# Split-float projections of a transformer block on one core: low part of the moving side by adding DMA, sums on VectorE, reversed values on ScalarE's queue

## The chip, the cores and the metric

The kernel runs on one NeuronCore of a Trainium2 chip. It computes one layer of a hybrid block for 1024 tokens of width 1024 in float32. The metric is device time in microseconds, from the first to the last instruction of one launch, with the little that lies around them. The kernel before takes 2165.42 us, the median of three runs (2165.0 to 2167.76).

## The reference

All is float32. `SEQ` and `D_MODEL` are 1024, `FF_HIDDEN` is 2816; there are 8 heads in the gated recurrence (`hgrn2_mixer`) and 16 in the stick-breaking attention.

```python
h = rms_norm(x, norm1_gain[layer])
proj = h @ w_in[layer]
hq, hf, hi, hg, sq, sk, sv, ga, gb = split_cols(proj, IN_SPLITS)
o_hg = hgrn2_mixer(hq, hf, hi, lower_bounds[layer])
o_hg = rms_norm(o_hg, hg_out_norm[layer]).reshape(b, s, HG_WIDTH)
o_hg = o_hg * jax.nn.sigmoid(hg.astype(jnp.float32))
y_hg = o_hg.astype(x.dtype) @ w_hg_out[layer]
...
o_sb = stick_breaking(q, k, v).transpose(0, 2, 1, 3).reshape(b, s, SB_WIDTH)
y_sb = o_sb.astype(x.dtype) @ w_sb_out[layer]
mixed = jax.nn.sigmoid(ga) * y_hg + jax.nn.sigmoid(gb) * y_sb
x = x + mixed @ w_o[layer]
h2 = rms_norm(x, norm2_gain[layer])
gate, up = split_cols(h2 @ w_ffn_in[layer], (FF_HIDDEN, FF_HIDDEN))
x = x + (jax.nn.silu(gate) * up) @ w_ffn_out[layer]
```

## The kernel before

**Numbers in two parts.** Every large product splits its operands into a high part (a cast to float32r) and a low part (the value less its high part) and makes three matmuls: high by high, high by low, low by high (`mm3`). For each operand somebody must make the two parts. There are two ways in the kernel. `split` casts on ScalarE and subtracts on an engine that is named (VectorE or GpSimd). `load_w` casts on ScalarE, writes the negated high part of the value with a second ScalarE pass (L118, `wl`), and lets a DMA on GpSimd's queue add the raw value to it in SBUF (L119).

**Stages, in the order of the program.** (1) The input is normalized and turned (`norm_x`, `turn_x`), while the first head's weights arrive. (2) The recurrence: for each of 8 heads `hg_head` makes the head's own small matmuls, woven between the projections of the next head. Values (`v`) are needed with every second token tile reversed: `hg_v` stores the raw rows to `d_v`, `turn_v` copies them reversed inside DRAM to `d_vr`, `load_v` reads them back into the odd tiles of `v`; the matmuls of `state` (L464) read them. (3) The stick-breaking attention, woven with its projections and with the gates' projections. (4) Three products (`w_hg_out`, `w_sb_out`, `w_o`), in the class `Product`. (5) The feed-forward input (`ffn_in`), (6) its output (`ffn_out`).

**The three products.** Each is cut into quarters and made with seven block products in place of eight (`SEQ43`, `SEQ34`), with sums and differences of quarters on either side (`A_STEPS` and `B_STEPS`, made in place by `sum_step`). One block product is a *job*: four tiles of 12 matmuls each, in four PSUM banks. While job n runs, job n+1 is prepared, by four steps that stand behind the tiles of job n: `stationary(0)`, `moving(0)`, `moving(1)`, `stationary(1)`. A stationary half is 128 x 1024 values for two tiles, in buffers `wh` and `wl`; a moving half is 128 x 1024 values for half of the inner dimension, in two buffers `u` that hold the halves of one job together. The job's first tile reads both moving halves, the second half from its seventh matmul on. Sums for the stationary side run on GpSimd (`a_sum`), the others on VectorE. When a tile is done it is added up on VectorE (L941) or copied by ScalarE; finished quarters are multiplied by a gate (L969) that is loaded just before. The third product adds to the input (`add_x1`, L981).

**Into the feed-forward.** The second norm's rows are turned (`turn_h2`) in 16 turns, eight woven into the last job, eight behind the first four of `ffn_in`'s block products. A turn scales a row tile on VectorE (`hn`, L1058), transposes it on TensorE (L1062), copies it out, and makes its part of the moving operands at once (`b_op`): number 1 or 2 for the first four tiles, 5 or 6 for the last four. Numbers 7, 3 and 4 are made later in one go (`b_rest`). `a_prep` makes the weights' operands six block products ahead, with sums and half of the subtractions on GpSimd. `(f, m)` below is block product m of column block f; the order starts (0,1), (0,2), (1,1), (1,2), (2,1), (2,2), (0,5), (0,6), (1,5), (0,7), (0,3), (0,4).

**What sets the order.** TensorE's order is written out by hand (`weave`, `run`). The other engines' orders come from the framework's scheduler, and every engine and every DMA queue works strictly in its order: an instruction that waits holds all behind it. Loads go through SyncE's queue, the two `wr` buffers of the weights among them.

Of the kernel before, what the change touches and what calls it, by code (L numbers as in the profile page):

```python
# [7 lines left out]
F32 = mybir.dt.float32  # L8
# [3 lines left out]
AF = mybir.ActivationFunctionType  # L12
ALU = mybir.AluOpType
# [3 lines left out]
P = 128  # L17
# [17 lines left out]
def hybrid_block(ctx, tc, x, norm1_gain, w_in, lb_logits, hg_out_norm, sb_q_norm, sb_k_norm,  # L35
                 w_hg_out, w_sb_out, w_o, norm2_gain, w_ffn_in, w_ffn_out,
                 c_ident, c_blk, c_lvl, c_base, out):
    nc = tc.nc
# [64 lines left out]
    d_x1 = dp.tile([NT, P, D], F32, name="d_x1")  # L103
    d_act = dp.tile([3, NF // 2, P, HS], F32, name="d_act")

    def load_w(src, k0, nk, c0, ncol, pool=None):
        raw = wp.tile([P, nk, ncol], F32, tag="wr", bufs=2, name="wr")
        if pool:
            both = pool(F32R, (P, 2, nk, ncol))
            hi, lo = both[:, 0], both[:, 1]  # L110
        else:
            hi = wp.tile([P, nk, ncol], F32R, tag="wh", name="wh")
            lo = wp.tile([P, nk, ncol], F32R, tag="wl", name="wl")
        dma = nc.sync.dma_start(raw, src[k0 * P:(k0 + nk) * P, c0:c0 + ncol].rearrange("(k p) n -> p k n", p=P))
        if src is w_hg_out and c0:
            order(dma, last["oh"][7 if c0 == P else -1])
        nc.scalar.copy(hi, raw)
        nc.scalar.activation(lo, raw, AF.Copy, scale=-1.0)  # L118
        nc.gpsimd.dma_start(lo.bitcast(F32).rearrange("p k n -> p (k n)"), raw.rearrange("p k n -> p (k n)"),  # L119
                            accum_op=ALU.add)  # L120
        return hi, lo

    blocks, loaded = [], []
# [240 lines left out]
        return proj_v(get, evac)  # L364

    def turn_v(h):
        nc.sync.dma_start(d_vr[h // 2], d_v[h // 2, :, ::-1, :])

    def load_v(h):
        for j in range(2):  # L370
            nc.sync.dma_start(hd[h + j]["v"][:, 1::2, :], d_vr[h // 2, :, :, j * P:(j + 1) * P].rearrange("a p c -> p a c"))

    def hg_gates(h):
        d = hd[h]
# [14 lines left out]
    def hg_head(h):  # L389
# [3 lines left out]
        e = {}  # L393

        def prep():
            sc = e["sc"] = hg.tile([P, S], F32, tag="sc", bufs=1, name="sc")
            nc.gpsimd.memset(sc, 0.0)
            kb = e["kb"] = hg.tile([P, S], F32, tag="kl", name="kb")
            qb = e["qb"] = hg.tile([P, S], F32, tag="kl", name="qb")
            c4 = c.rearrange("p (b l) -> p b l", l=4)  # L400
            nc.gpsimd.tensor_sub(qb.rearrange("p (b l) -> p b l", l=4), c4,
                                 c4[:, :, 1:2].broadcast_to([P, S // 4, 4]))
# [114 lines left out]
        def norm(half):  # L517
# [7 lines left out]
            nc.sync.dma_start(d_ohg[h][:, sl], r)  # L525

        return prep, [
            (0.86, lambda: (base(0), turn_v(h) if h % 2 == 0 else None)),
            (2.463, lambda: (base(1), level_prep(0))),
            (2.075, lambda: (across(), level_prep(1), load_v(h) if h % 2 == 0 else None)),  # L530
            (2.243, lambda: (level(0), level_prep(2))),
            (0.5, lambda: turn(0)),
            (1.257, lambda: turn(1)),
# [333 lines left out]
    def split(e, src, hi, lo):  # L867
        nc.scalar.copy(hi, src)  # L868
        e.tensor_sub(lo, src, hi.bitcast(F32))  # L869
# [9 lines left out]
    class Product:  # L879
# [17 lines left out]
        def prep(self, i):  # L897
            m = self.seq[i]
            sides = self.ops[i] = [], []

            def stationary(c):
                cols = slice(c * 256, (c + 1) * 256)
                raw = lambda q: self.raw("a", q)[:, :, cols]
                hi = wp.tile([P, 4, 256], F32R, tag="wh", name="wh")
                lo = wp.tile([P, 4, 256], F32R, tag="wl", name="wl")
                sides[0].append((hi, lo))
                sum_step(self.a_sum, A_STEPS, m, raw)
                split(nc.vector, raw(A_SRC[m]), hi, lo)

            def moving(c):  # L910
                if c == 0:
                    sides[1].extend((unit1(), unit1()))
                ks = slice(2 * c, 2 * c + 2)
                raw = lambda q: self.raw("b", q)[:, ks, :]
                sum_step(nc.vector, B_STEPS, m, raw)
                split(nc.vector, raw(B_SRC[m]), *(u[:, ks, :] for u in sides[1]))
            return [lambda: stationary(0), lambda: moving(0), lambda: moving(1), lambda: stationary(1)]

        def tile(self, i, j):
            m = self.seq[i]  # L920
# [79 lines left out]
    def load_x1(t):  # L1000
        if t % 2 == 0:
# [5 lines left out]
    SEQ43, SEQ34 = (1, 2, 5, 6, 7, 4, 3), (1, 2, 5, 6, 7, 3, 4)  # L1007
    phases = [
        Product(SEQ43, w_quarter(w_hg_out, lambda: unit1, False), o_quarter(d_ohg, lambda: unit1),
                accumulate(m1, lambda: unit2, finish_hg), nc.gpsimd),  # L1010
        Product(SEQ43, w_quarter(w_sb_out, lambda: unit2, False), o_quarter(d_osb, lambda: unit1),
                accumulate(mixed, lambda: unit1, finish_sb), nc.gpsimd),
        Product(SEQ34, lambda q: mixed[q // 10 + q % 10 * 10], w_quarter(w_o, lambda: unit2, True), add_x1,
                nc.gpsimd)]
    jobs = [(ph, i) for ph in phases for i in range(7)]

    def job_steps(n):
        ph, i = jobs[n]
        box = []

        def start():
            for ph2, i2 in jobs[n + 2:n + 3]:
                ph2.load(i2)
            box.extend(jobs[n + 1][0].prep(jobs[n + 1][1]) if n + 1 < len(jobs) else [lambda: None] * 4)
        steps = [(0.0, start)]
        for j in range(4):
            steps += ph.tile(i, j) + [(0.0, lambda j=j: box[j]())]
        return steps

    phases[0].load(0)  # L1030
# [21 lines left out]
    def turn_h2(t, g):  # L1052
        half, j = t // 4, t % 4
        q = 11 + 10 * g + half
        if j == 0:
            h2f[q] = unit1(F32)
        hn = mp.tile([P, HS], F32, tag="m2", name="hn")
        nc.vector.scalar_tensor_tensor(hn, x1s(t, g * HS, HS), rss[t], g2[:, 0, g * HS:(g + 1) * HS],  # L1058
                                       op0=ALU.mult, op1=ALU.mult)
        tp = pbank("pt")  # L1060
        for i in range(4):
            nc.tensor.transpose(tp[:, i * P:(i + 1) * P], hn[:, i * P:(i + 1) * P], ident)  # L1062
# [55 lines left out]
    a_done = []  # L1118
# [206 lines left out]
```

## Time and profile before

The profiled execution took 2166.08 us, of which its span is 2164.3 us.

| what | value |
|---|---|
| median of three runs | 2165.42 us |
| profiled execution's own time | 2166.08 us |
| its span | 2164.3 us |
| mean granted TensorE clock | 0.986 |
| VectorE busy | 1430.1 us (66%) |
| ScalarE busy | 1107.9 us (51%) |
| GpSimd busy | 627.6 us (29%) |
| moved by DMA | 228.96 MB |

How to read it: PE is TensorE's matmuls, PEld its weight loads, DVE is VectorE, ACT is ScalarE, POOL is GpSimd, SP is SyncE; a name with q behind it is the engine's queue. "pd L138 <- DVE u L869" is a matmul into tile pd, line 138, that waited until the VectorE instruction of line 869 into tile u was done; then come the total in us, how often, and the longest. In a timeline a row has the start and the length in us, engine, line, operation, tile written <- tiles read, sizes, and in brackets the engine's idle time before it and what ended that. In a table by windows a row has the stretch, its length, each engine's busy time with its instructions, the granted clock of TensorE (1.00 is full) and the busy share of the 16 DMA engines.

### The profile page before, as it was taken

The numbers are of one execution on the slowest core, as the hardware profiler recorded it, in microseconds if no ns is written. First come the engines' busy times: TensorE is split into PE (matmuls) and PEld (weight loads), VectorE is DVE, ScalarE is ACT, GpSimd is POOL, SyncE is SP. The second block draws the span as 40 slices with busy tenths as digits, with TensorE's granted clock in tenths as the row PEclk, the third lists the DMA queues.
The fourth block names the chain that finished last, engine by engine and source line by source line (L and its number), as shares of the span: only waits on it lengthen the run. The fifth ranks groups of instructions, "written<-read, shape, count | busy, mean of one in ns | idle before, by whom it ended". The sixth has DMA issues, their size and how long they took to land.

```text
span 2164.3 us, 29494 instructions
## 1 busy us (share of the span) xinstructions
PE 2049.3 (95%) x10981; PEld 1736.9 (80%) x10981; DVE 1430.1 (66%) x2128; ACT 1107.9 (51%) x1834; POOL 627.6 (29%) x612
## 2 busy tenths in 40 slices
PE   6999999999999999999999989989799999999999
PEld 6889798888877977878877777777688888887887
DVE  5374765747377787787787698999733333337975
ACT  5455444535376677776776554536433333333443
POOL 3232222423220220221120043142655555545000
PEclk9999999999999999999999999999899999999999
DMA  5433333443544344444434626512222322245221
GB/s 175 105 98 78 99 84 93 98 108 89 137 99 107 85 105 106 91 101 106 97 81 111 216 90 204 180 36 101 83 64 79 103 62 81 67 175 210 83 98 48
DMA packets 197360, 228.96 MB, mean 106 GB/s; under 512 B 10537, under 2 KB 133857, under 8 KB 197217
## 3 DMA queue, kind: packets, MB, share of 16 engines
q1 hardware_dynamic: 185840, 187.63, 27.8%
q0 software_dynamic: 10368, 37.75, 9.3%
q8 instruction: 86, 1.41, 0.3%
q10 hardware_dynamic: 1008, 1.70, 0.2%
q14 instruction: 58, 0.47, 0.1%
HBM read 134.51 MB, written 38.01 MB: 80 GB/s over the span
## 4 chain that ended last, share of the span: by engine, by line
PE 70%; DVE 18%; ACT 5%; issue 4%; DMA 3%; POOL 0%; SPq 0%; DVEq 0%; ACTq 0%; POOLq 0%
PE pd L137 15%; PE pd L138 15%; PE pd L139 15%; DVE kp L729 2%; PE pt L138 2%; PE pt L139 2%; PE pt L137 2%; PE pt L762 2%; DVE wl L869 2%; DVE u L865 2%; DVE u L869 2%; PE po L137 1%; PE po L139 1%; PE po L138 1%; DVE a L736 1%
## 5 line engine op out<-in xcount | busy, mean ns | idle before, releaser
L137 PE MATMUL pd<-hT,wh 128*128 128x512 f32 (+1 forms) x920 | 377.5, 410 | 2.1 <-ACT hT L186 2.1
L139 PE MATMUL pd<-hT,wl 128*128 128x512 f32 (+1 forms) x920 | 358.1, 389 | 4.3 <-DMA wl<-wr 4.3
L138 PE MATMUL pd<-hT,wh 128*128 128x512 f32 (+1 forms) x920 | 357.5, 389 | 0.2 <-DVE hT L187 0.2
L868 ACT CAST wh<-u 128x512 fp32r<-128x512 f32 (+1 forms) x280 | 183.8, 684 | 223.8 <-PE po L139 68.4
L139 PEld LDWEIGHTS pd<-hT,wl 128*128 128x128 f32 x920 | 175.0, 190 | 41.5 <-ACT rs L225 2.6
L138 PE MATMUL pd<-u,wh 128*128 128x512 f32 x496 | 194.4, 392 | 12.2 <-DVE u L869 12.2
L869 DVE TENSOR_TENSOR wl<-u,wh 128x512 fp32r<-128x512 f32 (+1 forms) x196 | 170.0, 903 | 53.2 <-ACT wh L868 48.5
L137 PE MATMUL pd<-u,wh 128*128 128x512 f32 x496 | 194.9, 393 | 0.7 <-ACT c L1173 0.7
L137 PEld LDWEIGHTS pd<-hT,wh 128*128 128x128 f32 x920 | 176.3, 192 | 23.6 <-ACT hT L186 2.5
L138 PEld LDWEIGHTS pd<-hT,wh 128*128 128x128 f32 x920 | 176.3, 192 | 21.4 <-DVE hT L187 0.5
L119 POOL DMA_DIRECT2D wl<-wr x72 | 63.6, 884 | 357.3 <-ACT wl L118 281.5
L865 POOL TENSOR_TENSOR u<-u,u 128x1024 f32<-128x1024 f32 (+1 forms) x46 | 106.5, 2333 | 189.0 <-DVE u L976 53.4
L729 DVE TENSOR_TENSOR_SCAN kp<-kp,dsel 128x512 f32<-128x512 f32 (+3 forms) x128 | 129.5, 1012 | 40.0 <-ACT kp L722 40.0
L138 PE MATMUL pd<-wl,hT 128*128 128x256 f32 x512 | 145.8, 285 | 4.6 <-DMA wl<-wr 4.6
L137 PE MATMUL pd<-wh,hT 128*128 128x256 f32 x512 | 149.0, 291 | 0.0
L139 PE MATMUL pd<-wh,hT 128*128 128x256 f32 x512 | 145.7, 285 | 0.0
L722 ACT ACTIVATE kp<-pz,rq 128x128 f32<-128x128 f32 (+2 forms) x192 | 113.0, 589 | 61.2 <-PE pz L718 52.6
L139 PE MATMUL pd<-u,wh 128*128 128x512 f32 x352 | 137.7, 391 | 0.0
L736 DVE TENSOR_TENSOR a<-a,kp 128x128 f32<-128x128 f32 (+2 forms) x192 | 110.3, 575 | 14.8 <-ACT kp L722 0.9
L138 PEld LDWEIGHTS pd<-u,wh 128*128 128x128 f32 x496 | 93.8, 189 | 32.8 <-DVE u L869 13.6
L722 ACT ACTIVATE a<-pz,rq 128x128 f32<-128x128 f32 (+2 forms) x192 | 113.0, 588 | 2.7 <-PE pt L762 2.7
L762 PE MATMUL pt<-ident,a 128*128 128x128 f32 x576 | 90.4, 277 | 24.4 <-DVE a L736 15.4
(264 smaller groups left out, 5137.2 us busy)
## 6 DMA issues: line engine op xcount, KB each, us to landing
wr<-in_w_in SPq DMA_DIRECT2D x72, 512.0 KB, 4.2
wl<-wr POOLq DMA_DIRECT2D x72, 512.0 KB, 4.6
u<-in_w_ffn_in SPq DMA_DIRECT2D x24, 512.0 KB, 5.4
wr<-in_w_ffn_in SPq DMA_DIRECT2D x20, 512.0 KB, 3.8
u<-in_w_ffn_out SPq DMA_DIRECT2D x10, 1024.0 KB, 7.4
d_act<-c SPq DMA_DIRECT2D x33, 256.0 KB, 2.1
u<-d_act SPq DMA_DIRECT2D x8, 1024.0 KB, 6.7
qh<-qh SPq DMA_DIRECT2D x48, 128.0 KB, 2.3
```

Of the source, the lines that this page charges most:

```text
L119: nc.gpsimd.dma_start(lo.bitcast(F32).rearrange("p k n -> p (k n)"), raw.rearrange("p k n -> p (k n)"), accum_op=ALU.add)
L137: nc.tensor.matmul(ps, lh, rh, start=start, stop=False, skip_group_check=adds)
L138: nc.tensor.matmul(ps, lh, rl, start=False, stop=False, skip_group_check=adds)
L139: nc.tensor.matmul(ps, ll, rh, start=False, stop=stop, skip_group_check=adds)
L722: last["sig"] = [nc.scalar.activation(t[:, 0:w], ps[:, 0:w], AF.Sigmoid, scale=rq[:, n_, col:col + 1]) for n_, t in enumerate((kp, a))]
L729: nc.vector.tensor_tensor_scan(rev, rev, dsel[:, HS - w:][:, ::-1], initial=0.0, op0=ALU.mult, op1=ALU.max)
L736: nc.vector.tensor_mul(a[:, 0:w], a[:, 0:w], kp[:, 1:w + 1])
L762: nc.tensor.transpose(tp[:, s * P:(s + 1) * P], a[:, b * P:(b + 1) * P], ident)
L865: e.tensor_tensor(raw(to), raw(a), raw(b), op=op)
L868: nc.scalar.copy(hi, src)
L869: e.tensor_sub(lo, src, hi.bitcast(F32))
```

## The change

Lines that are only a number of the source moved by 5 to 17 lines; the code that differs:

```diff
+    def rest_by_dma(lo, raw):
+        nc.scalar.activation(lo, raw, AF.Copy, scale=-1.0)
+        nc.gpsimd.dma_start(lo.bitcast(F32).rearrange("p k n -> p (k n)"), raw.rearrange("p k n -> p (k n)"),
+                            accum_op=ALU.add)
...
     def load_w(src, k0, nk, c0, ncol, pool=None):
...
-        nc.scalar.activation(lo, raw, AF.Copy, scale=-1.0)
-        nc.gpsimd.dma_start(lo.bitcast(F32).rearrange("p k n -> p (k n)"), raw.rearrange("p k n -> p (k n)"),
-                            accum_op=ALU.add)
+        last["loads"] = last.get("loads", 0) + 1
+        if last["loads"] <= 5:
+            nc.gpsimd.tensor_sub(lo, raw, hi.bitcast(F32))
+        else:
+            rest_by_dma(lo, raw)
...
     def turn_v(h):
-        nc.sync.dma_start(d_vr[h // 2], d_v[h // 2, :, ::-1, :])
+        nc.scalar.dma_start(d_vr[h // 2], d_v[h // 2, :, ::-1, :])
...
     def load_v(h):
         for j in range(2):
-            nc.sync.dma_start(...)
+            nc.scalar.dma_start(...)
...
         def prep():
+            if h % 2 == 0:
+                turn_v(h)
...
-            (0.86, lambda: (base(0), turn_v(h) if h % 2 == 0 else None)),
+            (0.86, lambda: (base(0), load_v(h) if h % 2 == 0 else None)),
             (2.463, lambda: (base(1), level_prep(0))),
-            (2.075, lambda: (across(), level_prep(1), load_v(h) if h % 2 == 0 else None)),
+            (2.075, lambda: (across(), level_prep(1))),
...
             def moving(c):
...
                 sum_step(nc.vector, B_STEPS, m, raw)
-                split(nc.vector, raw(B_SRC[m]), *(u[:, ks, :] for u in sides[1]))
-            return [lambda: stationary(0), lambda: moving(0), lambda: moving(1), lambda: stationary(1)]
+                hi, lo = (u[:, ks, :] for u in sides[1])
+                nc.scalar.copy(hi, raw(B_SRC[m]))
+                rest_by_dma(lo, raw(B_SRC[m]))
+            return [lambda: moving(0), lambda: moving(1), lambda: stationary(0), lambda: stationary(1)]
...
         for j in range(4):
-            steps += ph.tile(i, j) + [(0.0, lambda j=j: box[j]())]
+            steps += [(0.0, lambda j=j: box[j]())] + ph.tile(i, j)
...
             b_op(6 if g else 5, cut, nc.vector)
+            if g:
+                b_op(7, cut, nc.vector)
...
-        split(e, raw(B_SRC[m]), *(u[cut] for u in bop[m]))
+        if cut[2:]:
+            split(e, raw(B_SRC[m]), *(u[cut] for u in bop[m]))
+        else:
+            hi, lo = (u[cut] for u in bop[m])
+            nc.scalar.copy(hi, raw(B_SRC[m]))
+            rest_by_dma(lo, raw(B_SRC[m]))
...
-        sum_step(nc.gpsimd, A_STEPS, m, raw)
-        split(nc.vector if m in (1, 2, 4) else nc.gpsimd, raw(A_SRC[m]), both[:, 0], both[:, 1])
+        sum_step(nc.gpsimd if n > 22 else nc.vector, A_STEPS, m, raw)
+        split(nc.vector if m in (1, 2, 4) or n <= 22 else nc.gpsimd, raw(A_SRC[m]), both[:, 0], both[:, 1])
...
-    rest = {6: (7, nc.vector), 7: (3, nc.gpsimd), 9: (4, nc.vector)}
+    rest = {6: (3, nc.vector), 8: (4, nc.vector)}
```

The three `Product` phases also get `nc.vector` in place of `nc.gpsimd` for `a_sum`, and an ordering line in `load_w` for `w_hg_out` goes, which no call reached. TensorE's order of instructions is the same as before.

In words: (a) the first five weight loads of the program take their low part by a subtraction on GpSimd; (b) the reversed copy of the values and its loads move from SyncE's queue to ScalarE's, and one step earlier; (c) in the products the moving side is prepared first, its low part by negated copy and adding DMA, all sums are on VectorE, and each step stands ahead of its tile; (d) at the start of the feed-forward the sums and subtractions of the first 23 weight operands are on VectorE, moving operand 7 is made in the turns, and 3 and 4 take their low parts by adding DMA.

**The values of the third pair of heads.** On SyncE's queue before (`d_v` takes the rows of the pair as they are, `d_vr` the reversed ones, `wr` are weights for the next projections):

```order
L361 DMA d_v<-vs 128x256
L114 DMA wr<-in_w_in 128x8x128
L525 DMA d_ohg<-r 128x512
L367 DMA d_vr<-d_v 512x1x256
L114 DMA wr<-in_w_in 128x8x128 x2
L371 DMA v<-d_vr 128x4x128 x2
```

On ScalarE now, at the same place in the program (`wl` is the negated copy of a weight, `kq` an exponential of a level, `sc` the scores):

```order
L107 ACTIVATE wl<-wr 128x1024
L372 DMA d_vr<-d_v 512x1x256
L493 ACTIVATE kq<-kq 128x1024
L445 COPY sc<-pz 64x4x64 x2
L493 ACTIVATE kq<-kq 128x1024
L376 DMA v<-d_vr 128x4x128 x2
L120 CAST wh<-wr 128x1024
```

The loads of `v` stood behind two weight loads; now they stand behind two exponentials and two copies on another engine.

**The first product, around its second job.** On GpSimd before, the sums of the stationary side, in place on quarters of `w_hg_out` (one `u` number each):

```order
L865 TENSOR_TENSOR u_12375<-u_12375,u_12377 128x4x256 x2
L865 TENSOR_TENSOR u_12375<-u_12375,u_12231 128x4x256
L865 TENSOR_TENSOR u_12231<-u_12377,u_12375 128x4x256
L865 TENSOR_TENSOR u_12252<-u_12252,u_12375 128x4x256
```

On ScalarE now, for the moving side of the third job (`u_12454` takes the high part, `u_12455` the low one, of the sum in `u_12221`; `u_12397` is an output quarter, `m` a gate):

```order
L978 ACTIVATE m_12477<-m_12477 128x512
L978 ACTIVATE m_12498<-m_12498 128x512
L925 CAST u_12454<-u_12221 128x1024
L953 COPY u_12397<-po 128x512
L107 ACTIVATE u_12455<-u_12221 128x1024
L925 CAST u_12454<-u_12221 128x1024
L107 ACTIVATE u_12455<-u_12221 128x1024
L876 CAST wh<-u_12372 128x1024
```

GpSimd has no arithmetic left in the three products, only the adding DMAs; ScalarE has one pass more for each moving half, and these stand ahead of the casts for the stationary side.

**The start of the feed-forward.** On GpSimd before (`wr` and the `u` of three-part names are weights of `w_ffn_in`, `u_14499<-u_14285` is moving operand 3):

```order
L869 TENSOR_TENSOR wh<-wr,wh 128x512
L865 TENSOR_TENSOR wr<-wr 128x512 x3
L869 TENSOR_TENSOR wh<-wr,wh 128x512
L869 TENSOR_TENSOR wh<-u_14050,wh 128x512
L865 TENSOR_TENSOR u_14050<-u_14050 128x512 x3
L869 TENSOR_TENSOR wh<-wr,wh 128x512 x2
L869 TENSOR_TENSOR u_14499<-u_14285,u_14498 128x512 x4
```

On GpSimd now, from the last product's DMA on (`u_14518` is the low part of operand 3, `u_14568` of operand 4, `u_14287` and `u_14851` are weights for later column blocks):

```order
L108 DMA u_13967<-u_13487 128x1024 x2
L873 TENSOR_TENSOR u_14287<-u_14287 128x512
L108 DMA u_14518<-u_14322 128x512 x4
L108 DMA u_14568<-u_14115 128x512
L873 TENSOR_TENSOR wr<-wr 128x512
L108 DMA u_14568<-u_14115 128x512 x3
L873 TENSOR_TENSOR u_14851<-u_14851 128x512
```

On VectorE now, the end of the work that block product (0,6) waits for (`u_14308` is the sum of operand 7, `u_14096` that of 5 and then 6, `u_14332` the low part of 6):

```order
L873 TENSOR_TENSOR u_14096<-u_14308,u_14096 128x4x128
L873 TENSOR_TENSOR wr<-wr 128x512
L873 TENSOR_TENSOR u_14308<-u_14322,u_14308 128x4x128
L877 TENSOR_TENSOR u_14318<-u_14096,u_14317 128x4x128
L877 TENSOR_TENSOR wh<-wr,wh 128x512
L873 TENSOR_TENSOR u_14096<-u_14322,u_14096 128x4x128
L877 TENSOR_TENSOR u_14337<-u_14308,u_14336 128x4x128
L873 TENSOR_TENSOR wr<-wr 128x512
L877 TENSOR_TENSOR u_14332<-u_14096,u_14331 128x4x128 x4
```

Weights' sums and subtractions (`wr`, `wh`) that were GpSimd's now stand between the operands' parts on VectorE.

More of the change, by code (lines that the diff above doesn't have):

```diff
@@ L113, in load_w @@
             lo = wp.tile([P, nk, ncol], F32R, tag="wl", name="wl")
-        dma = nc.sync.dma_start(raw, src[k0 * P:(k0 + nk) * P, c0:c0 + ncol].rearrange("(k p) n -> p k n", p=P))
-        if src is w_hg_out and c0:
-            order(dma, last["oh"][7 if c0 == P else -1])
+        nc.sync.dma_start(raw, src[k0 * P:(k0 + nk) * P, c0:c0 + ncol].rearrange("(k p) n -> p k n", p=P))
         nc.scalar.copy(hi, raw)
-        nc.scalar.activation(lo, raw, AF.Copy, scale=-1.0)
-        nc.gpsimd.dma_start(lo.bitcast(F32).rearrange("p k n -> p (k n)"), raw.rearrange("p k n -> p (k n)"),
-                            accum_op=ALU.add)
+        last["loads"] = last.get("loads", 0) + 1
[3 more added lines that the diff above has]
+            rest_by_dma(lo, raw)
         return hi, lo
@@ L366, in turn_v @@
     def turn_v(h):
-        nc.sync.dma_start(d_vr[h // 2], d_v[h // 2, :, ::-1, :])
+        nc.scalar.dma_start(d_vr[h // 2], d_v[h // 2, :, ::-1, :])
     def load_v(h):
         for j in range(2):
-            nc.sync.dma_start(hd[h + j]["v"][:, 1::2, :], d_vr[h // 2, :, :, j * P:(j + 1) * P].rearrange("a p c -> p a c"))
+            nc.scalar.dma_start(hd[h + j]["v"][:, 1::2, :],
+                                d_vr[h // 2, :, :, j * P:(j + 1) * P].rearrange("a p c -> p a c"))
     def hg_gates(h):
@@ L1009, in hybrid_block @@
         Product(SEQ43, w_quarter(w_hg_out, lambda: unit1, False), o_quarter(d_ohg, lambda: unit1),
-                accumulate(m1, lambda: unit2, finish_hg), nc.gpsimd),
+                accumulate(m1, lambda: unit2, finish_hg), nc.vector),
         Product(SEQ43, w_quarter(w_sb_out, lambda: unit2, False), o_quarter(d_osb, lambda: unit1),
-                accumulate(mixed, lambda: unit1, finish_sb), nc.gpsimd),
+                accumulate(mixed, lambda: unit1, finish_sb), nc.vector),
         Product(SEQ34, lambda q: mixed[q // 10 + q % 10 * 10], w_quarter(w_o, lambda: unit2, True), add_x1,
-                nc.gpsimd)]
+                nc.vector)]
     jobs = [(ph, i) for ph in phases for i in range(7)]
```

## The prediction

> **What bounds the kernel now.** I read the page's busy times first, then the windows by stage, then TensorE's waits in each stage.
>
> ```profile
> PE 2049.3 (95%) x10981; PEld 1736.9 (80%) x10981; DVE 1430.1 (66%) x2128; ACT 1107.9 (51%) x1834; POOL 627.6 (29%) x612
> 1248.25:1483.78 235.53, 216.95 (x914) 176.33 (x913) 215.94 (x204) 112.11 (x153) 70.08 (x25) 0.96 0.35 120
> 1483.78:1547.44 63.66, 45.93 (x209) 36.12 (x208) 61.75 (x96) 41.62 (x89) 30.43 (x18) 0.87 0.28 94
> 1547.44:1960.00 412.56, 411.88 (x1817) 340.73 (x1816) 151.66 (x222) 153.01 (x260) 221.72 (x167) 1.00 0.31 100
> ```
>
> The columns of a window are its length, then PE, PEld, DVE, ACT and POOL with their instructions, the granted clock, the DMA share and GB/s. TensorE is busy 95% of the span, so an edit can only win where TensorE waits, or runs at half clock after waiting. The steady feed-forward (third window, 411.88 busy of 412.56) has nothing to give. The first window holds product jobs 1 to 19; there VectorE is busy 92% (215.94 of 235.53). The second holds the last product job, the turns and the first block products of `ffn_in`; VectorE is busy 97%.
>
> TensorE's waits, in four stretches (0 to 75, 75 to 600, then the two windows above):
>
> ```profile
> PE pd L138 <- DMA wl<-wr: 4.6, 1, 4.6
> PE pd L139 <- DMA wl<-wr: 4.3, 2, 2.4
> ...
> PE pt L464 <- DMA v<-d_vr: 11.3, 3, 4.0
> ...
> PE pz L137 <- DVE u L941: 9.6, 3, 5.9
> PE pz L137 <- DVE u L981: 3.5, 1, 3.5
> PE pd L138 <- DVE u L869: 2.4, 1, 2.4
> PE pt L137 <- DVE u L981: 2.4, 1, 2.4
> ...
> PE pd L138 <- DVE u L869: 9.8, 2, 9.1
> PE pt L1062 <- DVE hn L1058: 3.9, 2, 3.4
> PE pt L138 <- DVE u L869: 3.8, 1, 3.8
> ```
>
> Each part of the change aims at one of these groups: adding DMAs of the first weights (8.9), the reversed values (11.3), VectorE in the products (17.9 in these rows) and at the turns (17.5).
>
> A wait costs twice, since the granted clock falls behind it:
>
> ```profile
> 1274.38 0.63 PE L139 MATMUL pz<-u,wl 128*128 128x512 f32 x1
> 1274.80 0.63 PE L137 MATMUL pz<-u,wh 128*128 128x512 f32 x1
> 1550.18 0.39 PE L137 MATMUL pd<-u,wh 128*128 128x512 f32 x1
> 1552.90 0.39 PE L137 MATMUL pt<-u,wh 128*128 128x512 f32 x1
> ```
>
> The first two, just behind a wait of 5.9, stand 0.42 apart. The last two are the starts of two tiles at full clock: 12 matmuls in 2.72, so 0.227 each, and 10.88 for a job of four tiles. Of busy time at half clock some 45% is thus loss. Half-clock time in a window is 2 x (1 - clock) x length.
>
> **The change part by part**, against the profiled execution's 2166.1.
>
> *The first five weights (a).*
>
> ```profile
> 28.00:36.00 8.00, 5.62 (x36) 5.44 (x35) 7.69 (x20) 5.36 (x14) 3.30 (x3) 0.79 0.68 177
> 66.00:76.00 10.00, 5.37 (x27) 5.20 (x27) 6.99 (x4) 5.84 (x9) 7.42 (x5) 0.66 0.46 105
> 24.94 1.05 ACT L118 ACTIVATE wl<-wr 128x1024 fp32r<-128x1024 f32 x1
> L119 POOL DMA_DIRECT2D wl<-wr x72: 855/877/1164, 13.2 to 1196.0; - x72
> DMA to landing us min/median/max: 4.5/4.6/7.3
> L401 POOL TENSOR_TENSOR qb<-c 128x1024 f32<-128x1024 f32 x8 | 16.0, 2005 | 7.8 <-DVE c L387 7.8
> ```
>
> Before, a low part took a pass of 1.05 and a DMA that landed 4.5 to 7.3 after its issue (the row of L119, 72 of them): 5.6 to 8.4. A GpSimd operation of that shape takes 2.0 here; its subtraction is not in the trace, the nearest two-input row of GpSimd is 3.0 (L865, below). So a low part comes 2.6 to 6 earlier, which covers each wait of this group (longest 4.6): 8.9 go. Half-clock time is 3.4 and 6.8 in the two windows; of the second at most the 5.4 that are busy can lose, so at most 8.8 x 0.45 = 4.0 goes with the waits. GpSimd could slow VectorE's normalization in the same stretch (VectorE is busy 7.69 of 8). Bounds -6 (a third of the waits turns into one on GpSimd) to -12.9; I take **-10**.
>
> *Reversed values (b).*
>
> ```profile
> 221.83 10.99 SPq L114 DMA_DIRECT2D wr<-in_w_in  x2
> 232.87 1.12 SPq L371 DMA_DIRECT2D v<-d_vr  x2
> 224.68 0.73 ACT L437 COPY sc<-pz 64x256 f32<-64x256 f32 x2
> 232.00:244.00 12.00, 8.13 (x33) 6.95 (x32) 7.44 (x16) 1.77 (x3) 0.99 (x1) 0.72 0.31 89
> 356.00:364.00 8.00, 4.56 (x22) 3.95 (x21) 5.20 (x13) 1.06 (x1) 0.00 (x0) 0.79 0.46 130
> ```
>
> SyncE's queue held the loads of `v` for 11.0 behind two loads of `wr` that waited for buffers; they were issued at 232.87 and TensorE waited for their landing. On ScalarE's queue the loads stand behind two exponentials and two copies of `sc`, which end at about 225.4 (third row). They land some 7 earlier, and the longest wait is 4.0: all 11.3 go, three times. Half-clock time is 6.7 in the first of these windows and 3.4 in the second; the third pair's I take as the second's. Of these 13.5 I count 0.6 a time as still waiting: 11.7 x 0.45 = 5.3. ScalarE pays three issues a pair (the SPq row has 1.12 for two); it has slack there, 1.77 busy of 12 and 1.06 of 8. If an instruction ahead on ScalarE waits, all behind it on that engine waits too, `d_vr`'s copies included. Bounds -13 to -16.6; I take **-16**.
>
> *The products (c).* 19 jobs at 10.88 make 206.7 of 235.53: 28.8 could go, waits and half clock.
>
> ```profile
> L865 POOL TENSOR_TENSOR u<-u,u 128x1024 f32<-128x1024 f32 x24 | 72.6, 3038 | 166.3 <-DVE u L976 53.4 <-DMA u<-in_w_sb_out 49.8 <-DMA u<-in_w_hg_out 36.3
> L869 DVE TENSOR_TENSOR u<-u,u 128x1024 fp32r<-128x1024 f32 x42 | 58.2, 1402 | 11.3 <-ACT u L868 11.0
> L868 ACT CAST u<-u 128x1024 fp32r<-128x1024 f32 x42 | 43.0, 1048 | 36.8 <-DVE u L865 32.4 <-DVE u L869 1.9 <-DVE wl L869 1.3
> 1256.50 2.88 DVE L969 TENSOR_TENSOR u<-m,u 128x512 f32<-128x512 f32 x1
> 1262.64 0.68 DVE L969 TENSOR_TENSOR u<-m,u 128x512 f32<-128x512 f32 x1
> q0 software_dynamic: 10368, 37.75, 9.3%
> ```
>
> VectorE loses 42 subtractions of 1.4 (-58.2) and gets 24 sums of about 1.2, the uncontended length of such an operation (+29). GpSimd's sums of 3.0 go, and with them what the fourth row against the fifth shows: the same multiplication took 2.88 beside GpSimd and 0.68 alone. So VectorE's 215.94 falls by 29 at the least, 92% to 80% or lower, and its late sums, which end the waits above, come earlier.
>
> The price is on ScalarE and the DMAs. ScalarE gets about 40 negated copies of 1.05: 112 to 154, 65% of the window. Each adding DMA took 9.3% of 2164 / 72 = 2.8 of all 16 engines; two in a job of 10.88 are 51% on top of a share of 35%: **86% busy**. A chain for the first moving half is cast 1.05, a copy of 0.6 between, negation 1.05, landing 4.6: 7.3 behind the job's start, 8.5 with a sum of 1.2 ahead, and with the longest landing (7.3) 11.2, against 10.88. The second half's two passes end 2.1 later, at 4.8: 9.4 to 10.6, and 12.1 to 13.3 with the longest landing, against 10.88 + 6 x 0.227 = 12.24. So at usual landings both are hidden by 1.6 to 3; in bursts of loads they are not. Because the quarters are summed in place, the next sum of a quarter now waits for the DMA that reads it. Bounds: -28.8 (all), -5 (crowding gives most back); I take **-18**, nearer the good end, as landings of 72 had a median of 4.6.
>
> A rule speaks against this part. The Trainium skill, page "SBUF — State Buffer", section "SBUF: two separate sides", says that a DMA from GpSimd's queue has its descriptors written by GpSimd, which some VectorE operations lock out; by its example of 620 ns becoming 3100 ns, landings would by my estimate come 2.5 later, past 12.24 for the second half, so rival D below. The trace speaks rather against it: GpSimd's 72 issues took 0.86 to 1.16 each (row of L119), with VectorE 66% busy. The same page, "Who interferes with whom", counts operations with two inputs, which VectorE mostly has here, among those that do not stop the writing of descriptors, as an inference.
>
> *The turns (d).*
>
> ```profile
> 1498.48 0.39 PE L139 MATMUL po<-u,wl 128*128 128x512 f32 x1
> 1501.86 0.68 DVE L981 TENSOR_TENSOR u<-u,po 128x512 f32<-128x512 f32 x1
> 1542.88 0.79 PE L138 MATMUL pd<-u,wh 128*128 128x512 f32 x1 [9.11 <-DVE u L869]
> 1489.99 0.68 DVE L869 TENSOR_TENSOR u<-u,u 128x512 fp32r<-128x512 f32 x1
> 1490.59 0.74 DVE L1058 SCALAR_TENSOR_TENSOR hn<-u,rs,u 128x512 f32<-128x512 f32 x1
> ```
>
> From the last tile's sum (done at 1502.45) to the first matmul of (0,6) VectorE took 40.4. Undisturbed, an operation of 512 columns follows the next at 0.60 and a scaled row at 0.66 (last two rows). The order now puts 37 of the first and 6 of the second ahead of the last subtraction that (0,6) needs: 37 x 0.60 + 6 x 0.66 + 0.4 for the small ones = 26.6, so 13.8 less, though sums of weights and operand 7 stand on VectorE now: what goes is the time lost to GpSimd's work beside it. The last tile's sum itself came 3 late, and half-clock time shrinks by some 2: -19 at best. Five GpSimd operations stay in the stretch, and the adding DMAs for 3 and 4 have two block products of slack. Bounds -19 to -6; I take **-15**.
>
> The sum: -10 - 16 - 18 - 15 = -59: 2166.1 - 59 = **2107**. The profiled execution lies 0.7 above the median, within the runs' spread, so nothing is added for that. Attention, the steady feed-forward and the output are untouched.
>
> **The rivals.** *B: the moving side comes late in crowded jobs.* The 86% speaks for it, and landings up to 7.3; against it, that the mean share leaves room and the deadline is an entire job. The products then give nothing: 2166 - 41 = 2125. *C: VectorE is the bound at the turns*, as the sums of 23 weights and operand 7 join it where it is 97% busy: -6 in place of -15, and about as much lost in the products from its sums: 2116 to 2120. *E: the loads of `v` are held on ScalarE's queue* by an exponential that waits for its sum, so the wait stays: 2107 + 16 = 2123, near 2121 if a little goes. *D: slower.* If the landings in the products are above 12.24 - 4.8 = 7.4 in every job, TensorE waits for the second half each time; a wait of 1.5 and half clock behind it (1.6 of loss, as one period of 3.4 at 45%) is 3 in 20 jobs, +60: 2166 - 41 + 60 = 2185. Only the longest of 72 landings comes near it, but none of those was in a stage this crowded.
>
> **How the numbers follow.** The forecast 0.58, B 0.23, C 0.08, E 0.05, D 0.06. The best ends of all parts make -77, the worst -30: 2089 to 2136, which holds B, C and E as well and leaves out D and a little. Faster by over 0.2% (about what a measurement of this kernel can tell from no change): all but D, 0.94. D is slower in 0.05 and within 0.2% in 0.01, where only half its jobs are late.
>
> **What would show it.** Right: no wait of L139 for `wl` before 75; none at L464; no GpSimd arithmetic and VectorE near 80% in the products; the waits for `u` at L941 and L981 gone; the first matmul of (0,6) within 30 of the last tile's sum; a mean clock above 0.986. Wrong: product jobs whose first tile waits for a DMA into `u`, landings above 7.4 there, or VectorE still above 90%.

## The result, and the profile after

The changed kernel takes 2147.24 us, median of four runs (2144.05 to 2149.9), beside 2166.02 for the kernel before (2165.0 to 2167.76): a ratio of 0.9912, 95% interval 0.9895 to 0.9929. It is faster by 18.8, where 59 had been forecast, and lies outside the range (2089 to 2136). The profiled execution took 2149.9, its span 2148.1.

The same two stretches as before (from and to the same matmuls, as TensorE's order is unchanged): first jobs 1 to 19 of the products, then the last job, the turns and the first block products of `ffn_in`.

```profile
1224.25:1473.49 249.24, 221.44 (x913) 177.42 (x912) 162.32 (x193) 147.88 (x194) 32.95 (x38) 0.94 0.78 203
1473.49:1522.76 49.27, 43.28 (x210) 35.16 (x208) 47.30 (x97) 40.45 (x87) 5.65 (x5) 0.93 0.36 104
```

The jobs that took 235.53 now take 249.24, though VectorE fell from 92% busy to 65% (162.32 of 249.24). What rose is the DMA share, 0.35 to 0.78. The second stretch fell from 63.66 to 49.27. Where the time went, by the start of the same matmul in the two traces:

| stretch (matmuls on TensorE, counted) | before | after | change |
|---|---|---|---|
| start to 500 | 100.91 | 90.55 | -10.4 |
| to 3600 (values; end of the recurrence) | 525.90 | 513.41 | -12.5 |
| to 7185 (attention, first job) | 621.44 | 620.29 | -1.2 |
| to 8097 (jobs 1 to 19) | 235.53 | 249.24 | +13.7 |
| to 8305 (last job, turns, up to (0,6)) | 63.66 | 49.27 | -14.4 |
| to 8380 (operands 3 and 4) | 17.02 | 25.44 | +8.4 |
| to the last | 595.78 | 595.85 | +0.1 |

The sum, -16.2, is the difference of the two profiled executions (2166.08 and 2149.9). TensorE's waits, in the recurrence, in jobs 1 to 19, and in the last two stretches up to 1545:

```profile
PE pz L507 <- DVE kq L497: 4.4, 4, 1.1
...
PE pd L142 <- ACT wh L876: 5.5, 2, 4.7
PE pd L143 <- DMA u<-u: 5.1, 2, 3.6
PE pt L143 <- DMA u<-u: 4.1, 3, 2.3
PE pd L142 <- DVE u L991: 4.1, 1, 4.1
PE pz L144 <- DVE wl L877: 3.9, 1, 3.9
PE pt L142 <- DVE u L951: 2.7, 1, 2.7
PE pz L142 <- ACT wh L876: 1.9, 1, 1.9
...
PE pt L1072 <- DVE hn L1068: 3.8, 1, 3.8
PE pd L143 <- DVE u L877: 2.2, 2, 1.7
...
PE pd L143 <- DMA u<-u: 5.4, 3, 3.8
```

The waits for `wl` in the first 75 us and for `d_vr` are gone; a small one for `kq` is new. In the products three kinds share the wait: the adding DMA itself (`u<-u`, 9.2), the stationary side (`wh` and `wl`, 11.3), and sums of finished tiles (L951, L991, 6.8). In the last line TensorE waits for the adding DMAs of operands 3 and 4.

### The profile page after: what moved, and what is told of

It is laid out like the page before. It is cut to its first block, busy times and chain, and to the rows that moved or that the text cites. A ratio compares the mean times of both kernels' runs of the same rounds, so it can differ in the third digit from the quotient of the medians.

```text
span 2148.1 us, 29624 instructions
## 1 busy us (share of the span) xinstructions
PE 2045.9 (95%) x10981; PEld 1730.3 (81%) x10981; DVE 1364.0 (63%) x2130; ACT 1143.5 (53%) x1879; POOL 559.0 (26%) x610
## 4 chain that ended last, share of the span: by engine, by line
PE 67%; DVE 15%; DMA 7%; ACT 6%; issue 4%; POOL 0%; SPq 0%; DVEq 0%; ACTq 0%; POOLq 0%
PE pd L142 15%; PE pd L143 15%; PE pd L144 15%; DVE kp L737 3%; PE pt L144 2%; PE pt L142 2%; PE pt L143 2%; PE pt L770 2%; DMA u<-u 2%; DVE a L744 2%; DVE wl L877 1%; PE pz L507 1%; PE po L142 1%; PE po L787 1%; PE po L144 1%
## 5 line engine op out<-in xcount | busy, mean ns | idle before, releaser
L877 DVE TENSOR_TENSOR wl<-u,wh 128x512 fp32r<-128x512 f32 (+1 forms) x196 | 164.1, 873 | 85.0 <-ACT wh L876 82.8
L143 PE MATMUL pd<-u,wh 128*128 128x512 f32 x496 | 197.5, 398 | 12.7 <-DMA u<-u 10.5
L142 PE MATMUL pd<-u,wh 128*128 128x512 f32 x496 | 198.0, 399 | 10.3 <-ACT wh L876 5.5
L108 POOL DMA_DIRECT2D wl<-wr x67 | 59.0, 880 | 312.6 <-ACT wl L107 240.6
L144 PE MATMUL pd<-u,wh 128*128 128x512 f32 x352 | 138.4, 393 | 0.0
L873 DVE TENSOR_TENSOR u<-u,u 128x512 f32<-128x512 f32 (+1 forms) x130 | 110.3, 883 | 42.7 <-DMA u<-u 13.1
L143 PEld LDWEIGHTS pd<-u,wh 128*128 128x128 f32 x496 | 95.4, 192 | 35.7 <-issue 6.3
L142 PEld LDWEIGHTS pd<-u,wh 128*128 128x128 f32 x496 | 95.4, 192 | 31.7 <-ACT wh L876 6.4
```

The lines of the kernel that those rows point to most:

```text
L142: nc.tensor.matmul(ps, lh, rh, start=start, stop=False, skip_group_check=adds)
L143: nc.tensor.matmul(ps, lh, rl, start=False, stop=False, skip_group_check=adds)
L144: nc.tensor.matmul(ps, ll, rh, start=False, stop=stop, skip_group_check=adds)
L873: e.tensor_tensor(raw(to), raw(a), raw(b), op=op)
```

## The experiments

Each run has its own runs of the kernel before beside it; in brackets stand the ratio to these and its 95% interval.

**The early parts alone.** (a) and (b) kept; products and feed-forward as before.

```diff
-                hi, lo = (u[:, ks, :] for u in sides[1])
-                nc.scalar.copy(hi, raw(B_SRC[m]))
-                rest_by_dma(lo, raw(B_SRC[m]))
-            return [lambda: moving(0), lambda: moving(1), lambda: stationary(0), lambda: stationary(1)]
+                split(nc.vector, raw(B_SRC[m]), *(u[:, ks, :] for u in sides[1]))
+            return [lambda: stationary(0), lambda: moving(0), lambda: moving(1), lambda: stationary(1)]
...
-        sum_step(nc.gpsimd if n > 22 else nc.vector, A_STEPS, m, raw)
+        sum_step(nc.gpsimd, A_STEPS, m, raw)
...
-    rest = {6: (3, nc.vector), 8: (4, nc.vector)}
+    rest = {6: (7, nc.vector), 7: (3, nc.gpsimd), 9: (4, nc.vector)}
```

> Parts (a) and (b) alone; the products and the start of the feed-forward as before. If the losses of the changed kernel lie in the products (13.7 longer there by the traces) and the rest is independent, this run gains what its trace gained ahead of the products, 24: 2166 - 24 = 2142, faster than the whole change. If the early part only shifts waits into the products (a rival: less time for the loads that the products need), the gain is well below 20.

Measured 2141.39 (0.9891, 0.9876 to 0.9906). The early parts alone are worth 22.6 beside the 2163.96 of the kernel before in the same set, near the 24 that their trace had promised. The rest of the change takes some 5 of it back: 5.9 by the times, 4.5 by the ratios, whose intervals overlap. The rival that waits were only shifted falls.

**The low part of the moving side on VectorE.**

```diff
-                hi, lo = (u[:, ks, :] for u in sides[1])
-                nc.scalar.copy(hi, raw(B_SRC[m]))
-                rest_by_dma(lo, raw(B_SRC[m]))
+                split(nc.vector, raw(B_SRC[m]), *(u[:, ks, :] for u in sides[1]))
```

> The changed kernel with the low part of the products' moving side by a VectorE subtraction, as before, and all else kept (moving side first, all sums on VectorE). Theory T1, the adding DMAs cost the time (late landings, sums in place that wait until the DMA has read, loads made late by a busy share of 0.79): the products lose their 13.7 and more, 2120 to 2134. Theory T2, the stationary side behind the moving side is what comes late: it stays at 2145 to 2150. Theory T3, sums at the head of VectorE's queue wait for loads and hold the evictions: 2140 or above, since these sums stay and 42 subtractions join them.

Measured 2104.84 (0.972, 0.9704 to 0.9736), 42 below the changed kernel and below what any theory gave. Its jobs 1 to 19:

```profile
1223.24:1429.96 206.72, 206.72 (x913) 171.17 (x912) 197.16 (x225) 113.82 (x154) 0.00 (x0) 1.00 0.40 136
```

TensorE is busy for all of 206.72, at full clock: nothing waits, although VectorE is 95% busy (197.16). So all 28.8 that the products could give is there, and the adding DMAs of this stage turn it into a loss.

**The sums back on GpSimd, with the adding DMAs; the old order, with the adding DMAs.**

```diff
-                accumulate(m1, lambda: unit2, finish_hg), nc.vector),
+                accumulate(m1, lambda: unit2, finish_hg), nc.gpsimd),
...
-                nc.vector)]
+                nc.gpsimd)]
```

> The changed kernel with the stationary side's sums of the three products back on GpSimd, ahead of the same adding DMAs in its queue. T3 (sums on VectorE hold its queue): 2125 to 2138. T1: no gain or a loss, 2145 to 2165, since sums of 3.0 stand among the issues of the adding DMAs and slow VectorE. T2: within 4 of 2147.

```diff
-            return [lambda: moving(0), lambda: moving(1), lambda: stationary(0), lambda: stationary(1)]
+            return [lambda: stationary(0), lambda: moving(0), lambda: moving(1), lambda: stationary(1)]
...
-            steps += [(0.0, lambda j=j: box[j]())] + ph.tile(i, j)
+            steps += ph.tile(i, j) + [(0.0, lambda j=j: box[j]())]
```

> The changed kernel with the old order of the products' steps (a stationary half, both moving halves, a stationary half), each behind its tile again; adding DMAs and sums on VectorE kept. T2: 2125 to 2138, the waits for the stationary casts and subtractions (L876, L877, 11.8 in all) go. T1: slower, 2155 to 2185, since the adding DMAs are issued a tile or two later and land after the job has begun.

Measured 2174.32 (1.0043, 1.0031 to 1.0055) and 2152.75 (0.9947, 0.9932 to 0.9962). Both are slower than the changed kernel, so T2 and T3 fall. T1 had the sign of both; it had put the first too low by 9 and the second too high by 2.

**Which part of the change holds the gain.** The same two edits on the run with VectorE's low parts.

> The run with VectorE's low parts in the products (2104.8), with the stationary side's sums back on GpSimd. It differs from the kernel with parts (a) and (b) alone (2141.4, products as before) by the new order of the steps and by the start of the feed-forward. If moving the sums to VectorE is what took the 28.8 out of the products, the products lose most of it: 2125 to 2138. If the order did: 2104 to 2112.

> The run with VectorE's low parts in the products (2104.8), with the old order of the steps, each behind its tile, and all sums on VectorE. If the order took the 28.8 out of the products: 2125 to 2138. If the sums did: 2104 to 2112.

Measured 2130.83 (0.9849, 0.9832 to 0.9865) and 2106.07 (0.9732, 0.9718 to 0.9747). The sums' move to VectorE holds 26 (with the adding DMAs in place it held 27, 2174.32 beside 2147.24); the order of the steps nothing that can be measured. With the sums on GpSimd (its groups in jobs 1 to 19, in line form: count, then total and mean ns):

```profile
L873 POOL TENSOR_TENSOR u<-u,u 128x1024 f32<-128x1024 f32 x22 | 66.1, 3022 | 130.8 <-issue 50.9 <-DMA u<-in_w_sb_out 46.0 <-DVE wl L877 33.5
L877 DVE TENSOR_TENSOR wl<-u,wh 128x1024 fp32r<-128x1024 f32 x39 | 54.5, 1397 | 6.8 <-ACT wh L876 3.9 <-issue 2.6
L873 DVE TENSOR_TENSOR u<-u,u 128x1024 f32<-128x1024 f32 x22 | 37.9, 1730 | 1.5 <-DMA u<-d_osb 1.4
```

and with them on VectorE:

```profile
L873 DVE TENSOR_TENSOR u<-u,u 128x1024 f32<-128x1024 f32 x43 | 51.5, 1220 | 2.8 <-DMA u<-d_osb 2.4 <-DMA u<-in_w_sb_out 0.3
L877 DVE TENSOR_TENSOR wl<-u,wh 128x1024 fp32r<-128x1024 f32 x38 | 46.3, 1221 | 1.7 <-ACT wh L876 1.5
```

VectorE's own operations take 1397 and 1730 ns on average while GpSimd has sums to make, and 1221 and 1220 when it has none. Twice the sums cost VectorE 13.6 more, and all else on it becomes cheaper. The Trainium skill, page "SBUF — State Buffer", section "Who interferes with whom", says that a VectorE operation with two inputs in SBUF contends with a GpSimd operation that reads SBUF; these rows agree.

**What of the adding DMAs costs: first try.** Idle copies and DMAs, whose result nothing reads, were put on top of the run with VectorE's low parts; the second run reads the raw quarter in place of the high part.

```diff
+    junk = [wp.tile([P, 2, HS], F32R, tag="wr", bufs=2, name="junk") for _ in range(2)]
...
+                nc.scalar.activation(junk[c], raw(B_SRC[m]), AF.Copy, scale=-1.0)
+                nc.gpsimd.dma_start(junk[c].bitcast(F32).rearrange("p k n -> p (k n)"),
+                                    hi.bitcast(F32).rearrange("p k n -> p (k n)"), accum_op=ALU.add)
```

> The run with VectorE's low parts in the products (2104.8), and on top of it the changed kernel's negated copies and adding DMAs at the same places, of the same size, into two buffers that nothing reads; they read the high part, which no sum overwrites. It adds the traffic and the passes alone. Crowding theory (a DMA share near 0.8 makes the loads late): 2125 to 2147. Dependence theory (what costs is that matmuls and sums wait for these DMAs): 2104 to 2112.

> As the run before, but the idle DMAs read the raw quarter, as in the changed kernel: the next sum in place of that quarter has to wait until they have read it. No matmul waits for their result. If sums that wait are most of the loss: 2130 to 2150. If the matmuls' own wait for the landing is: within 5 of the run before.

Measured 2149.79 (0.9938, 0.9923 to 0.9953) and 2158.75 (0.9974, 0.9965 to 0.9984). The first is inconclusive: ScalarE's wait row for its idle copies

```profile
ACT junk L926 <- DMA junk<-u: 48.2, 18, 6.1
```

shows a wait that the changed kernel doesn't have, as the two idle buffers are used again in each job. The difference of the two runs stands: about 9 when the idle DMAs read the raw quarter, which the next sum overwrites. That was neither forecast: too much for "within 5", and far from most of the loss. By which wait the 9 come is not shown; VectorE waits for an idle DMA only once in that trace, for 1.8.

**Traffic alone, passes alone.**

The first run keeps the idle DMAs alone, into two buffers that are set to zero once; the second keeps the idle copies alone.

```diff
+        nc.gpsimd.memset(u.bitcast(F32), 0.0)
...
+                nc.gpsimd.dma_start(junk[c].bitcast(F32).rearrange("p k n -> p (k n)"),
+                                    hi.bitcast(F32).rearrange("p k n -> p (k n)"), accum_op=ALU.add)
```

```diff
+                nc.scalar.activation(junk[c], raw(B_SRC[m]), AF.Copy, scale=-1.0)
```

> The run with VectorE's low parts in the products (2104.8), and adding DMAs of the same number and size from the high parts into two buffers that nothing reads, without the negated copies, which in the run of idle DMAs made ScalarE wait 48 for the DMA of the job before. Only GpSimd's queue waits for these DMAs, so this is their traffic and nothing else. If traffic alone makes the loss: 2130 to 2150. If most of the loss was ScalarE or VectorE waiting for the adding DMAs themselves: 2105 to 2118.

> The run with VectorE's low parts in the products (2104.8), with the negated copies of 1.05 on ScalarE (42 more passes) into two buffers that nothing reads, and no DMA. ScalarE was busy 116 of 209 there, so by slack alone: 2104 to 2108. If the passes hold ScalarE's queue ahead of the stationary casts at the wrong moment: 2112 or more.

Measured 2140.58 (0.9893, 0.9878 to 0.9908) and 2105.92 (0.973, 0.9716 to 0.9745). DMAs whose result nothing reads cost 36; the 42 passes cost nothing that can be measured. In jobs 1 to 19 with the idle DMAs: the window, the two main queues, the landing of the loads (median us from issue to landing, last number), and ScalarE's waits for the gates.

```profile
1223.25:1456.49 233.24, 215.99 (x914) 172.58 (x913) 198.47 (x218) 111.06 (x149) 32.99 (x38) 0.97 0.84 213
...
q0 software_dynamic: 5587, 20.33, 46.9%
q1 hardware_dynamic: 18150, 29.24, 36.5%
...
u<-d_osb SPq DMA_DIRECT2D x16, 256.0 KB, 7.0
m<-d_gb SPq DMA_DIRECT2D x16, 256.0 KB, 8.8
...
ACT m L979 <- DMA m<-d_ga: 36.2, 9, 10.4
ACT m L979 <- DMA m<-d_gb: 36.0, 9, 13.1
```

Without them:

```profile
u<-d_osb SPq DMA_DIRECT2D x16, 256.0 KB, 3.9
m<-d_gb SPq DMA_DIRECT2D x16, 256.0 KB, 2.6
...
ACT m L976 <- DMA m<-d_gb: 21.4, 10, 3.9
ACT m L976 <- DMA m<-d_ga: 12.3, 6, 2.7
```

At a DMA share of 0.84 the ordinary loads land late: a quarter's piece at 7.0 in place of 3.9, a gate from `d_gb` at 8.8 in place of 2.6. ScalarE stands 72 in place of 34 at the gates, and the stationary casts stand behind it in its queue.

Not all of the 36 is the price of traffic in the products. The two profiled executions lie 31 apart: jobs 1 to 19 take 26.5 more (233.24 beside 206.72), the stretch behind them 7.7 more (56.84 beside 49.17). In those jobs neither TensorE nor VectorE nor ScalarE waits for an idle DMA, so the 26.5 is traffic. The idle buffers, though, are the two that the first weights of `ffn_in` need, and SyncE's queue stood for them near the end of the jobs and once behind:

```profile
SPq L1117 <- DMA junk<-u: 21.2, 2, 18.0
```

Whether the 7.7 come from that was not tried; the idle copies hold the same buffers and lose nothing. The changed kernel's jobs lie 42.5 over 206.72. The other 16 would then be what waits for the adding DMAs themselves; that is a difference of two runs and was not tried apart.

**Half the traffic.**

```diff
+                if c == 1:
+                    split(nc.vector, raw(B_SRC[m]), hi, lo)
+                    return
```

> The changed kernel with the adding DMA for the first moving half of each job alone, the second half's low part by VectorE: half the traffic. If the cost grows with the traffic in proportion: about 2126, midway between 2104.8 and 2147. If it comes from the second half's later landing or from the queue filling up past some point: 2104 to 2115.

Measured 2119.0 (0.9796, 0.9781 to 0.981): 14 of the 42. Its jobs 1 to 19:

```profile
1223.17:1441.18 218.01, 210.33 (x913) 171.76 (x912) 178.25 (x206) 130.10 (x173) 16.50 (x19) 0.99 0.64 180
```

They take 218.01 at a DMA share of 0.64, 11.3 over the undisturbed 206.72, where the changed kernel lies 42.5 over it at 0.78. With half the adding DMAs there is about a quarter of the cost, between the two forecasts and nearer to the second. The run leaves out the DMAs of the second half, so less traffic and the waits that go with that half are not told apart.

**Through which wait.** In the first of these two runs the sigmoid of the gates is left out: the products are multiplied by the raw gate.

```diff
-        nc.sync.dma_start(g, src[n][:, h * HS:(h + 1) * HS])
-        last["gate"] = nc.scalar.activation(g, g, AF.Sigmoid)
+        gd = nc.sync.dma_start(g, src[n][:, h * HS:(h + 1) * HS])
+        act = nc.scalar.activation(tmp("sig"), last["resident"], AF.Sigmoid)
+        order(act, gd)
+        last["gate"] = act
...
+    rest = wp.tile([P, 2, HS], F32, tag="wr", bufs=2, name="rest")
+    nc.gpsimd.memset(rest, 0.0)
+    last["resident"] = rest[:, 0, :]
```

> The changed kernel with ScalarE's 32 sigmoid passes of the gates over a tile that is always there, instead of the gate just loaded; VectorE multiplies with the raw gate, so the sigmoid of the gates is left out. The gates' loads, their buffers, all other traffic and ScalarE's passes stay; what goes is that ScalarE stands at a gate's load (60 us in the changed kernel) with the stationary casts behind it. If that is the way by which the traffic costs most: 2115 to 2130. If VectorE's and TensorE's waits for the adding DMAs and the quarters' loads carry it: 2140 to 2148.

The second gives the gates more buffers.

```diff
-        g = mp.tile([P, HS], F32, tag="m2", name="m2")
+        g = wp.tile([P, 2, HS], F32, tag="wr", bufs=2, name="m2")[:, 0, :] if last.setdefault("g", 0) % 5 > 2 else mp.tile([P, HS], F32, tag="m2", name="m2")
+        last["g"] += 1
...
```

> The changed kernel with five buffers in rotation for the gates instead of three (two weight buffers that are idle there; the first weights of the feed-forward load later for that), so that gates can be asked for earlier. If the late gates cost and can be had earlier: 2125 to 2140. If the DMAs are full, so that an earlier request only takes the place of another load: 2143 to 2155.

Measured 2139.61 (0.9884, 0.9861 to 0.9907) and 2146.82 (0.9917, 0.9899 to 0.9935). The first is 8 below the changed kernel by the times and 6 by the ratios, whose intervals overlap: ScalarE's stand at the gates is not most of the cost. Part of the wait only moved, as VectorE now waits 10.6 for raw gates. More buffers for the gates change nothing that can be measured. With ScalarE freed, TensorE's longest waits in jobs 1 to 19 are these:

```profile
PE pz L144 <- DVE wl L877: 8.5, 1, 8.5
PE pd L144 <- DVE wl L877: 6.4, 1, 6.4
PE pt L142 <- DVE u L951: 4.7, 1, 4.7
PE pt L143 <- DMA u<-u: 3.3, 2, 3.0
PE pd L143 <- DMA u<-u: 3.2, 1, 3.2
```

VectorE's operations are now late, behind sums that wait for DMAs. Just ahead of the first two of these waits, in this order, VectorE stood so, for an adding DMA and for a load of weights:

```profile
1295.02 1.23 DVE L873 TENSOR_TENSOR u<-u,u 128x1024 f32<-128x1024 f32 x1 [12.43 <-DMA u<-u]
1397.86 1.23 DVE L873 TENSOR_TENSOR u<-u,u 128x1024 f32<-128x1024 f32 x1 [9.30 <-DMA u<-in_w_o]
```

No single wait was found that carries the cost. Which share each queue has stays open.

**The version that beats both.** VectorE's low parts in the products, and for operands 3 and 4 as well.

```diff
-        if cut[2:]:
-            split(e, raw(B_SRC[m]), *(u[cut] for u in bop[m]))
-        else:
-            hi, lo = (u[cut] for u in bop[m])
-            nc.scalar.copy(hi, raw(B_SRC[m]))
-            rest_by_dma(lo, raw(B_SRC[m]))
+        split(e, raw(B_SRC[m]), *(u[cut] for u in bop[m]))
```

> The run with the moving side's low part by VectorE in the products (2104.8), and operands 3 and 4 of the feed-forward by VectorE subtractions too, so that the change has no adding DMA left but those of the weights. In the trace of that run TensorE waits 4.8 and 1.1 for those adding DMAs, with 6.8 of half clock. If that is a cost of the DMAs: 2096 to 2100. If VectorE's eight more subtractions of 0.6 come late instead: 2103 to 2108.

Measured 2098.04 (0.9697, 0.9683 to 0.9712): 7 below the run without this edit, 49 below the changed kernel.

## Why the prediction was wrong

**The first weights (a):** forecast -10, measured -10.4. Right.

**The values (b):** forecast -16, measured -12.5. The wait for `d_vr` went. The term was mis-sized by 3.5: the new wait for `kq` (4.4, four times 1.1) was not in it. It stands in VectorE's order, where the multiplications that the levels' matmuls need now follow two others and a copy (L448, L450, L320) that were behind the first of them. I had looked for a price on ScalarE alone. This is read from the traces and not tried.

**The products (c):** forecast -18, measured +13.7; here the prediction failed. What it said of VectorE held: the sums off GpSimd free it, and that is worth 26, though 6.8 of waits for its sums stayed in the changed kernel. The step that failed is "I take -18, nearer the good end, as landings of 72 had a median of 4.6". Those landings were mostly of stages with a DMA share near 0.4. The prediction had itself worked out 86% for the products, and still used the landing of the emptier stages. In the changed kernel's products the landing is

```profile
u<-u POOLq DMA_DIRECT2D x38, 512.0 KB, 7.0
```

and the longest took 10.9; 17 of the 38 came later than 7.4. In the prediction's own chain a landing of 7.0 in place of 4.6 puts the second half at 11.8 to 13.0, against its deadline of 12.24.

And it had priced only that deadline of the moving side: TensorE waits 9.2 for it, while traffic with no deadline at all costs 26.5 in the same jobs. The other loads pay for the share too (a quarter's piece lands at 7.6 in the changed kernel, at 3.9 without the adding DMAs), and the engines that wait for those loads hold their queues. The sums in place, which the prediction says must wait for the DMA that reads the quarter, had no price in the sum; in jobs 1 to 19 they did wait:

```profile
DVE u L873 <- DMA u<-u: 13.1, 4, 4.8
```

The bound for crowding, -5, reached no further than giving the gain back; the runs show that it goes past it. Rival D had the right mechanism, late landings in crowded jobs, with too narrow a path, 0.06 of chance and a price of 60 in the products, where 13.7 was measured; it asked for late landings in every job. Rival B had the same mechanism and put the products at nothing.

The rule that I weighed there, of the Trainium skill's page "SBUF — State Buffer", section "SBUF: two separate sides", speaks of GpSimd kept from writing descriptors. The trace doesn't show that: its issues took

```profile
L108 POOL DMA_DIRECT2D u<-u x38 | 33.0, 867 | 189.7 <-ACT u L107 121.2 <-PE pt L143 15.1 <-DVE wl L877 13.4
```

0.87 each, as in the kernel before. The landings became late with the share of the DMA engines: the idle DMAs, at a share of 0.84, landed at 6.6.

**The turns (d):** forecast -15. Up to (0,6) it was -14.4, by the path that was counted, but with the stretch behind it the part gave only 6.0. What failed is "the adding DMAs for 3 and 4 have two block products of slack": they cost 8.4, and the run without them gained 7. GpSimd's queue after the change shows something in their way:

```profile
1525.58 0.86 POOL L108 DMA_DIRECT2D u<-u  x1 [4.52 <-DVE u L873]
1529.10 1.73 POOL L873 TENSOR_TENSOR wr<-wr 128x512 f32<-128x512 f32 x1 [2.67 <-DVE c L1192]
1530.78 2.68 POOL L108 DMA_DIRECT2D u<-u  x3
```

A sum for later weights stood ahead of the last three adding DMAs, waited 2.7 for VectorE and took 1.7. I had counted the operations left on GpSimd and not looked for who stands behind them. How much of the 8.4 is this sum and how much the landing of the DMAs was not tried apart.

**The sum.** That the run with VectorE's low parts comes to 2104.8, near the forecast of 2107, doesn't make the forecast right: there the products gave 28.8 and the turns 5.4. Nor does rival C's price of 2116 to 2120 follow from its own words: -6 in place of -15 makes 2116, and as much lost again in the products makes 2125.

## What to carry to other kernels

Price added traffic at the DMA share that it makes, and for every load of the stage, not only for the transfer's own deadline; a landing time from an emptier stage says little. An experiment with the same DMAs into a buffer that nobody reads separates traffic from dependence, as long as that buffer is taken from nobody. And when work is put on a queue, list what else stands in that queue at that place, the operation left behind too.

## What the runs showed of the hardware

By the two queue rows of the run with idle DMAs, 20.33 MB of adding DMAs took 46.9% of the engines' 233.24 us, 5.4 us a MB, and the 29.24 MB of the other queue, nearly all loads, took 36.5%, 2.9 us a MB: a byte added in SBUF took the DMA engines 1.85 times as long as one of these. And VectorE at 95% busy, alone, holds TensorE less than at 65% behind late loads: how busy an engine is says less than what stands at the head of its queue.
